# Sums with PSUM tiles of their own between projection and FFN, a shorter look-ahead there, and one empty unit in the first attention head

## The chip, the cores and the metric

The kernel runs on one core of one Trainium2 chip. The metric is the time of one execution on the device in microseconds (us), the median of several runs. One execution was recorded by the hardware profiler; all times of single instructions come from that one, counted in us from its first instruction. The engines are called PE (matrix products), PEld (its weight loads), DVE (vector engine), ACT (scalar engine), POOL (the general engine) and SP (here it only issues transfers).

## What is computed

One layer of a diffusion backbone on 384 tokens (128 context, 256 latent) of width 2048, all in float32:

```python
mod = silu(cond) @ w_ada + b_ada                 # six modulation vectors
h = rmsnorm(x) * (1 + sc1) + sh1
q, k, v, g, lr_f, lr_b, fo = split(h @ w_in)
la = log_sigmoid(lr @ w_a2 + b_a) / 16           # decays of each head, two directions
o = gla(q, k, v, la, states)                     # 4 heads, chunks of 64 tokens
f = real(fft2(fo))
m = (sigmoid(h @ w_gate + b_gate) halves: g_a * (o' @ w_br_gla) + g_b * (f @ w_br_four)) @ w_out
x = x + ga1 * rmsnorm(m)
h = rmsnorm(x) * (1 + sc2) + sh2
ff = (silu(h @ w_ffn_gate) * (h @ w_ffn_up)) @ w_ffn_down
x = x + ga2 * rmsnorm(ff)
```

## The kernel before

Activations lie transposed: a tile of 128 channels by T = 384 tokens, 16 such tiles (KT) for the width 2048. Every large product is made of three passes with operands split in a high and a low part (`hi*hi + hi*lo + lo*hi`, `gemm`, L254). A product of one output tile (`proj`, L263) takes two halves of 8 input tiles, each 24 matmuls of 128x384. Before each half `grab` takes a pair of split weights that lies ready and pushes a new one: a transfer on SP (`load`, L191), a cast on ACT (L224) and a subtraction on DVE (L225). The pairs are used three halves after they were pushed.

The order of instructions on PE, ACT, DVE and POOL is written out by hand (`manual_schedule`, L129): each engine executes its instructions in the order in which the program emits them. An instruction that waits holds up everything emitted behind it on its engine. Only SP's order is left to the scheduler.

**Gate products and GLA.** The loop at L817 makes 32 products of `w_gate`. After each half of a product it takes one step of a side job (`side`, L809): one unit of `gla()` and one of the modulation job `ada_rest` (two DVE operations L556 in most units). In the second half of a product the destination (`gate`, L818: ACT adds the bias and writes `gz`, L820; SP stores it) is emitted ahead of that step. `gla()` has 14 units for each of the four heads, cut by `yield`: unit 1 transposes k on PE (L635); unit 2 is the product for the decays, `z` (L650); unit 3 makes the decays from it, a chain over ACT (Abs L657, Exp L658, Ln L659), DVE (L661), ACT (cast `lah`, L284) and DVE (`lal`, L285); units 4 and 5 sum them on PE (`bT`, L671, and `sx`, L677) for the two directions and take their exponentials on ACT; units 6 to 14 do attention, states and outputs. Unit 1 of head 0 follows the first half of product 0. As 14 is even, each unit number keeps its place to first or second halves in all heads: unit 2 comes behind a second half and its `gz`, unit 3 behind a first half, unit 4 behind a second one. The loop has 64 steps; the four heads and three closing units take 59.

**From projection to FFN.** The loop at L1064 makes the 16 tiles of the output projection. `wout` (L1034) keeps running sums over the tiles in `qs[0..2]`: of squares, of the gated product with x, and of squares of the gated product. For the last tile `wout_last` (L1048) forms its terms straight from the product in PSUM, ACT and DVE by turns. Then `wide_sum` (L1101) sums over channels by matmuls with ones of 64 columns, DVE and ACT make two scale factors per token from the sums, and `rows2` (L1109) spreads each over 128 partitions (`prow`, `prow2`). With them `res_m` (DVE, L1133) and `res_a` (POOL, for tile 0 DVE, L1137) form the new x1, tile by tile, and `res_b` and `res_c` the input h2 of the FFN in a high and a low part: DVE, ACT, DVE. The first three FFN products are computed side by side while the tiles arrive (the "head", L1188 to L1204, 9 matmuls for each tile, L1201). `res_m` and `res_a` run LAG = 3 tiles ahead. After tiles 9 and 12 of that loop POOL gets a weight subtraction of 128x1024 (L1206). Three tiles (0, 9, 12) take a "fused" form in which the context and latent segments are scaled separately (L1161, L1165).

**The end.** `tok_sum` (L288) sums the squares of the FFN's output with one column of ones (L292); from them come the last scale, and 16 output tiles (L1278 to L1330).

PSUM is handed out from two pools of banks: `psm` (3, tag `mm`) and `pss` (5, tag `side`).

Of the kernel before, what the change touches and what calls it, by code (L numbers as in the profile page):

```python
# [96 lines left out]
def tile_step(ctx: ExitStack, tc: tile.TileContext, a, o):  # L97
# [498 lines left out]
    with ExitStack() as s:  # L596
# [23 lines left out]
        def gla():  # L620
# [10 lines left out]
            for h in range(NH):  # L631
# [30 lines left out]
                lah, lal = (pg.tile([P, 3, 2, P], F32R, tag=t, name=t) for t in ("lah", "lal"))  # L662
                split_act(lah, lal, la)
                yield
                for d in range(2):


                    bT = pss.tile([P, T], F32, tag="side", name="bT")
                    for t in range(3):
                        for j, l in enumerate((lah, lal)):  # L670
                            PE.matmul(  # L671
                                bT[:, t * P : (t + 1) * P], l[:, t, d], tri[:, d * P : (d + 1) * P],
                                start=j == 0, stop=j == 1,
                            )
# [344 lines left out]
    with ExitStack() as s:  # L1019
# [40 lines left out]
        rate[0] = 0.6  # L1060
        spare_h = ((pe, "hid_hi", 2), (pe, "hid_lo", 2))
# [2 lines left out]
        for i in range(KT):  # L1064
            p = psm.tile([P, T], F32, tag="mm", name="pmm")
            for g in range(2):
                n = 2 * i + g - 2 * KT
                if n < -6:
                    w = grab()
                else:  # L1070

                    w = take()
                    if raw2 is None:
                        raw2 = adap.tile([P, 2, G], F32, tag="adacc", name="raw2")
                    if n <= -4:
                        load(raw2[:, n % 2, :])
                    if n <= -5:
                        load()
                    split()
                    if -4 <= n <= -2:  # L1080
                        split(spare_w if n == -3 else spare_h)
                    if n >= -4:
                        load()
                    if n == -4:
                        load(raw2[:, 1, :])
                gemm(p, w, mT, 8, k0=8 * g, first=g == 0, last=g == 1)
                if g:
                    if i < KT - 1:
                        wout(p, i)
                    else:  # L1090
                        sq0, sq2 = wout_last(p, i)
# [9 lines left out]
        def wide_sum(dst, src):  # L1101
            for t in range(3):
                PE.matmul(dst[:, t, :], src[:, t * P : (t + 1) * P], ones[:, 0:64], start=True, stop=True)

        r = pe.tile([P, 2, 3], F32, name="r12", bufs=1)
        u = pe.tile([P, 2, 3], F32, name="u12", bufs=1)
# [9 lines left out]
        DVE.tensor_copy(u[:, 0, :], pst[0][:, 0, :, 0])  # L1116
# [4 lines left out]
        DVE.tensor_add(qs[2], qs[2], sq2)  # L1121
        wide_sum(pst[1][:, 1], qs[2])
        rows2(prow, 0)
        DVE.scalar_tensor_tensor(u[:, 0, :], pst[1][:, 1, :, 0], 0.5, r[:, 0, :], op0=ALU.mult, op1=ALU.mult)
        DVE.tensor_add(u[:, 0, :], u[:, 0, :], pst[1][:, 0, :, 0])
        DVE.scalar_tensor_tensor(u[:, 1, :], u[:, 0, :], 2.0 / D, r[:, 0, :], op0=ALU.mult, op1=ALU.mult)
        DVE.tensor_add(u[:, 1, :], u[:, 1, :], msx)

        t1s = {}

# [4 lines left out]
        def res_a(k):  # L1135

            (POOL if k else DVE).tensor_add(x1(k), t1s.pop(k), x1(k))  # L1137

        res_m(0)
        rsqrt(r[:, 1, :], u[:, 1, :], 1.0)  # L1140
        rows2(prow2, 1)
        for k in range(3):
            if k:
                res_m(k)
            res_a(k)
        for lo, hi, c in segs:
            DVE.tensor_scalar_mul(mg32(KT - 1)[:, lo:hi], p[:, lo:hi], mods[:, 2, KT - 1, c : c + 1])

        h2 = alloc_A()
        hp = [  # L1150
            (pss if u == 0 else psm).tile([P, T], F32, tag="mm" if u else "side", name="pmm") for u in range(HEAD)
        ]
        zt = [pss.tile([P, T], F32, tag="side", name="z") for _ in range(2)]
        fused = (0, 9, 12)

        def res_b(k):

            z = zt[k % 2]
            if k in fused:
                for lo, hi, c in segs:  # L1160
                    DVE.scalar_tensor_tensor(  # L1161
                        z[:, lo:hi], x1(k)[:, lo:hi], mods[:, 4, k, c : c + 1], prow2[:, lo:hi],
                        op0=ALU.mult, op1=ALU.mult,
                    )
                    ACT.activation(h2[0][:, k, lo:hi], z[:, lo:hi], AF.Identity, bias=mods[:, 3, k, c : c + 1])  # L1165
# [9 lines left out]
        def res_c(k):  # L1175
            z = zt[k % 2]
            if k in fused:
                for lo, hi, c in segs:
                    DVE.scalar_tensor_tensor(
                        h2[1][:, k, lo:hi], z[:, lo:hi], mods[:, 3, k, c : c + 1], h2[0][:, k, lo:hi].bitcast(F32),  # L1180
                        op0=ALU.add, op1=ALU.subtract,
                    )
# [104 lines left out]
        DVE.tensor_copy(r3, pst[:, 0:3])  # L1287
        DVE.tensor_add(r3, r3, pys[0][:, 0:3])
        rsqrt(r3, r3, 1.0 / D)
        put(pe_ks[0], psm, "mm")  # L1290
        for t in range(3):
# [117 lines left out]
```

## Time and profile before

| what | value |
|---|---|
| median of 3 runs | 2034.52 us (2034.43 to 2035.05) |
| the profiled execution, its own time | 2032.79 us |
| its span, first to last instruction | 2031.0 us |
| mean granted TensorE clock | 0.997 |
| busy DVE, ACT, POOL | 1251.2, 770.4, 34.2 us |

The page gives busy times and shares of the span; the view of waits says which engine sat idle until what; the timeline lists merged instructions with their start, their length and, in brackets, the idle time before them with what ended it; the view of windows gives for each stretch the busy time of each engine with the number of instructions, and the granted clock of TensorE, 1.00 for full speed.

### The profile page before, as it was taken

Reading aid. Unit: us, or ns where it says so; the run is one execution under the profiler, and the core shown is the slowest. Engines: PE = TensorE matmul, PEld = TensorE weight load, DVE = VectorE, ACT = ScalarE, POOL = GpSimd, SP = SyncE. Lnnn points to the kernel's source line nnn. Section 1 sums busy time; section 2 is a strip of 40 time slices with the busy share of each in tenths; the row PEclk is TensorE's granted clock in tenths of the full one; section 3 lists DMA queues with packets and bytes.
Section 4 is the critical chain, followed back from the end, with each engine's and each line's share of the span. In section 5 each row is a group of like instructions: output and inputs, shape, how many; then the busy total and the mean of one; then the engine's idle time right before and its main releaser. Section 6 shows DMA issues by size and latency. Waiting matters only on the chain.

```text
span 2031.0 us, 30079 instructions
## 1 busy us (share of the span) xinstructions
PE 2014.6 (99%) x12236; PEld 1959.9 (96%) x12236; DVE 1251.2 (62%) x1655; ACT 770.4 (38%) x1144; POOL 34.2 (2%) x46
## 2 busy tenths in 40 slices
PE   8999999999999999989999999999999999999999
PEld 5779999999999999989999999999999999999998
DVE  5669787898677778866444545453545454544345
ACT  4233545443346544446233222222222222222235
POOL 0000000000000000002000000000000000000001
PEclk9999999999999999999999999999999999999999
DMA  9978677767546785533444444443444444433332
GB/s 390 371 254 276 206 239 233 246 223 261 210 154 207 256 282 185 193 125 115 145 148 147 151 146 147 151 148 125 145 145 146 147 149 150 138 133 125 126 130 97
DMA packets 112395, 373.94 MB, mean 184 GB/s; under 512 B 13692, under 2 KB 32316, under 8 KB 108160
## 3 DMA queue, kind: packets, MB, share of 16 engines
q1 hardware_dynamic: 111248, 370.64, 53.2%
q8 instruction: 96, 1.57, 0.3%
q10 hardware_dynamic: 1008, 1.38, 0.2%
q14 instruction: 43, 0.35, 0.0%
HBM read 358.34 MB, written 13.63 MB: 183 GB/s over the span
## 4 chain that ended last, share of the span: by engine, by line
PE 98%; ACT 1%; DVE 1%; issue 0%; DMA 0%; ACTq 0%; DVEq 0%
PE pmm L258 67%; PE pdn L258 18%; PE pv L399 3%; PE pf L258 2%; PE pgm L382 1%; PE pmm L1201 1%; PE px L417 1%; PE px L300 0%; PE po L629 0%; PE pr L564 0%; PE py L1278 0%; PE pgm L496 0%; PE dl L629 0%; PE pp L856 0%; PE px L870 0%; PE bT L671 0%
## 5 line engine op out<-in xcount | busy, mean ns | idle before, releaser
L258 PE MATMUL pmm<-A_hi,whi 128*128 128x384 f32 x2480 | 831.8, 335 | 0.0
L258 PE MATMUL pmm<-A_hi,wlo 128*128 128x384 f32 x2480 | 828.9, 334 | 0.0
L258 PE MATMUL pmm<-A_lo,whi 128*128 128x384 f32 x2480 | 828.8, 334 | 0.0
L225 DVE TENSOR_TENSOR wlo<-raw,whi 128x1024 fp32r<-128x1024 f32 x434 | 529.8, 1223 | 416.8 <-ACT whi L224 415.6
L224 ACT CAST whi<-raw 128x1024 fp32r<-128x1024 f32 x436 | 457.5, 1050 | 582.4 <-PE pmm L258 226.9
L258 PEld LDWEIGHTS pmm<-A_hi,whi 128*128 128x128 f32 x2480 | 465.6, 188 | 2.9 <-issue 1.8
L258 PEld LDWEIGHTS pmm<-A_lo,whi 128*128 128x128 f32 x2480 | 465.7, 188 | 0.2
L258 PEld LDWEIGHTS pmm<-A_hi,wlo 128*128 128x128 f32 x2480 | 465.6, 188 | 0.0
L556 DVE SCALAR_TENSOR_TENSOR adacc<-adaw,spad,adacc 128x1024 f32<-128x1024 f32 x240 | 296.9, 1278 | 1.2 <-DMA adaw<-in_w_ada 1.0
L258 PE MATMUL pdn<-hid_hi,whi 128*128 128x384 f32 x704 | 235.2, 334 | 0.0
L258 PE MATMUL pdn<-hid_hi,wlo 128*128 128x384 f32 x704 | 235.1, 334 | 0.0
L258 PE MATMUL pdn<-hid_lo,whi 128*128 128x384 f32 x704 | 235.1, 334 | 0.0
L258 PEld LDWEIGHTS pdn<-hid_hi,whi 128*128 128x128 f32 x704 | 132.2, 188 | 0.4 <-issue 0.4
L258 PEld LDWEIGHTS pdn<-hid_lo,whi 128*128 128x128 f32 x704 | 132.2, 188 | 0.0
L258 PEld LDWEIGHTS pdn<-hid_hi,wlo 128*128 128x128 f32 x704 | 132.2, 188 | 0.0
L284 ACT CAST hid_hi<-hfE 128x384 fp32r<-128x384 f32 x44 | 22.6, 513 | 164.0 <-DVE hfE L1224 164.0
L1224 DVE TENSOR_TENSOR hfE<-sg,pmm 128x384 f32<-128x384 f32 x44 | 24.4, 555 | 84.6 <-PE pmm L258 84.0
L1216 ACT ACTIVATE sg<-pmm 128x384 f32<-128x384 f32 x44 | 21.6, 492 | 136.3 <-PE pmm L258 136.2
L1241 DVE TENSOR_TENSOR Blo<-Blo,pdn 128x384 f32<-128x384 f32 x72 | 39.5, 553 | 47.9 <-PE pdn L258 47.9
L1241 DVE TENSOR_TENSOR Bhi<-Bhi,pdn 128x384 f32<-128x384 f32 x72 | 39.1, 549 | 34.1 <-PE pdn L258 34.0
L258 PE MATMUL pmm<-o_hi,whi 128*128 128x384 f32 x128 | 42.8, 335 | 0.0
L258 PE MATMUL pmm<-o_lo,whi 128*128 128x384 f32 x128 | 42.8, 334 | 0.0
(309 smaller groups left out, 1520.9 us busy)
## 6 DMA issues: line engine op xcount, KB each, us to landing
adaw<-in_w_ada SPq DMA_DIRECT2D x128, 512.0 KB, 3.9
raw<-in_w_g SPq DMA_DIRECT2D x88, 512.0 KB, 3.2
raw<-in_w_u SPq DMA_DIRECT2D x88, 512.0 KB, 3.3
raw<-in_w_d SPq DMA_DIRECT2D x88, 512.0 KB, 3.2
slab<-in_w_ada SPq DMA_DIRECT2D x32, 1024.0 KB
raw<-in_w_gate SPq DMA_DIRECT2D x64, 512.0 KB, 4.5
raw<-in_w_in SPq DMA_DIRECT2D x44, 512.0 KB, 3.2
raw<-in_w_out SPq DMA_DIRECT2D x32, 512.0 KB, 4.5
```

What stands on the lines that cost most here:

```text
L224: ACT.copy(hi, raw)
L225: sub = lambda: eng.tensor_sub(lo, raw, hi.bitcast(F32))
L258: PE.matmul(dst, w[wi][:, k * n + n0 : k * n + n0 + P], x[xi][:, k0 + k, :], start=first and k == 0 and j == 0, stop=last and k == kts - 1 ...
L284: ACT.copy(hi, src)
L382: PE.matmul(pgv[q : q + 32, :], spad[:, k, :], slab[k // (KT // 2)][:, k % (KT // 2), :], start=k < 4, stop=k >= KT - 4,)
L399: PE.matmul(pv[2 * t + g], hT[x_][:, kb, t * P : (t + 1) * P], w_[:, g * 512 : (g + 1) * 512], start=kb == 0 and j == 0, stop=kb == KT - 1 ...
L417: PE.matmul(px, w_[:, u * P : (u + 1) * P], hT[x_][:, kb, :], start=j == 0, stop=j == 2)
L556: DVE.scalar_tensor_tensor(acc[:, c, :], w, spad[:, k, c : c + 1], acc[:, c, :], op0=ALU.mult, op1=ALU.add,)
L1201: PE.matmul(hp[u], hw[u][j][:, ((k - 1) % 8) * P : ((k - 1) % 8 + 1) * P], h2[m][:, k - 1, :], start=k == 1 and j == m == 0, stop=k == KT ...
L1216: ACT.activation(sgs[j], p, AF.Silu)
L1224: DVE.tensor_mul(hf, sgs.pop(j), p)
L1241: DVE.tensor_add(acc(k), acc(k), p)
```

## The change

In head 0 of `gla()` an empty unit follows the decay chain, so that `bT` and all that follows, in this head and the others, comes one step later. In the step from projection to FFN the last tile takes the way of the others (ACT writes `mg32`, squares it, DVE multiplies), but its terms are not added into `qs`: they get products of their own, and the four groups of sums (running and last, first and second factor) get four PSUM tiles. Small matmuls of ones by ones (`narrow_warm`) are put behind `prow` (2) and behind `prow2` (4); their result is never read. LAG becomes 2. In tile 0 the two segments go to different PSUM tiles (`zx` is new, from `psm`). At the end `tok_sum` is replaced by `wide_sum`.

```diff
                 split_act(lah, lal, la)
                 yield
+                if h == 0:
+                    yield
                 for d in range(2):
...
             for lo, hi, c in segs:
-                g = mods[:, 2, i, c : c + 1]
-                DVE.scalar_tensor_tensor(pr[:, lo:hi], p[:, lo:hi], g, x1(i)[:, lo:hi], op0=ALU.mult, op1=ALU.mult)
-                ACT.activation(sq2[:, lo:hi], p[:, lo:hi], AF.Square, scale=g)
-            DVE.tensor_add(qs[1], qs[1], pr)
-            return sq0, sq2
+                ACT.mul(mg32(i)[:, lo:hi], p[:, lo:hi], mods[:, 2, i, c : c + 1])
+            ACT.activation(sq2, mg32(i), AF.Square)
+            DVE.tensor_mul(pr, mg32(i), x1(i))
+            return sq0, pr, sq2
...
-        pst = [pss.tile([P, 2, 3, 64], F32, tag="side", name=f"pst{n}") for n in range(2)]
+        E0, S0, E12, S12 = (pss.tile([P, 2, 3, 64], F32, tag="side", name="pst") for _ in range(4))
...
-        wide_sum(pst[0][:, 0], qs[0])
-        DVE.tensor_copy(u[:, 0, :], pst[0][:, 0, :, 0])
-        wide_sum(pst[0][:, 1], sq0)
-        DVE.tensor_add(u[:, 0, :], u[:, 0, :], pst[0][:, 1, :, 0])
+        wide_sum(E0[:, 0], qs[0])
+        wide_sum(S0[:, 0], last3[0])
+        for n in (1, 2):
+            wide_sum(E12[:, n - 1], qs[n])
+        for n in (1, 2):
+            wide_sum(S12[:, n - 1], last3[n])
+        DVE.tensor_copy(e[:, 0, :], E0[:, 0, :, 0])
+        DVE.tensor_add(u[:, 0, :], e[:, 0, :], S0[:, 0, :, 0])
         rsqrt(r[:, 0, :], u[:, 0, :], 1.0 / D)
-        wide_sum(pst[1][:, 0], qs[1])
-        DVE.tensor_add(qs[2], qs[2], sq2)
-        wide_sum(pst[1][:, 1], qs[2])
         rows2(prow, 0)
...
+        def narrow_warm(n):
+            for _ in range(n):
+                PE.matmul(hp[1][:, 0:P], ones, ones, start=True, stop=True)
+
+        narrow_warm(2)
         res_m(0)
-        rsqrt(r[:, 1, :], u[:, 1, :], 1.0)
+        rsqrt(r[:, 1, :], u[:, 0, :], 1.0)
         rows2(prow2, 1)
-        for k in range(3):
+        narrow_warm(4)
+        LAG = 2
+        for k in range(LAG):
             if k:
                 res_m(k)
             res_a(k)
-        for lo, hi, c in segs:
-            DVE.tensor_scalar_mul(mg32(KT - 1)[:, lo:hi], p[:, lo:hi], mods[:, 2, KT - 1, c : c + 1])
...
+        zx = psm.tile([P, T], F32, tag="mm", name="zx")
...
+        def z_of(k, lo):
+
+            return zx if k == 0 and lo else zt[k % 2]
...
-        LAG = 3
...
-        tok_sum(pst[:, 0:3], qs[0], *late)
-        tok_sum(pys[0][:, 0:3], last_sq)
+        pst, ps2 = (t.rearrange("p (t c) -> p t c", t=3)[:, :, 0:64] for t in (pst, pys[0]))
+        wide_sum(pst, qs[0], *late)
+        wide_sum(ps2, last_sq)
```

More of the change, by code (lines that the diff above doesn't have):

```diff
@@ L1095, in tile_step, with wide_sum @@
                     pass
-        pst = [pss.tile([P, 2, 3, 64], F32, tag="side", name=f"pst{n}") for n in range(2)]
-        def wide_sum(dst, src):
+        E0, S0, E12, S12 = (pss.tile([P, 2, 3, 64], F32, tag="side", name="pst") for _ in range(4))
+        def wide_sum(dst, *src):
             for t in range(3):
-                PE.matmul(dst[:, t, :], src[:, t * P : (t + 1) * P], ones[:, 0:64], start=True, stop=True)
+                for n, x in enumerate(src):
+                    PE.matmul(
+                        dst[:, t, :], x[:, t * P : (t + 1) * P], ones[:, 0:64], start=n == 0, stop=n == len(src) - 1,
+                    )
         r = pe.tile([P, 2, 3], F32, name="r12", bufs=1)
-        u = pe.tile([P, 2, 3], F32, name="u12", bufs=1)
+        e = pe.tile([P, 3, 3], F32, name="e12", bufs=1)
+        u = pe.tile([P, 3, 3], F32, name="u12", bufs=1)
         prow, prow2 = (pss.tile([P, T], F32, tag="side", name="prow") for _ in range(2))
@@ L1113, in rows2 @@
                 )
-        wide_sum(pst[0][:, 0], qs[0])
-        DVE.tensor_copy(u[:, 0, :], pst[0][:, 0, :, 0])
-        wide_sum(pst[0][:, 1], sq0)
-        DVE.tensor_add(u[:, 0, :], u[:, 0, :], pst[0][:, 1, :, 0])
+        wide_sum(E0[:, 0], qs[0])
[6 more added lines that the diff above has]
+        DVE.tensor_add(u[:, 0, :], e[:, 0, :], S0[:, 0, :, 0])
         rsqrt(r[:, 0, :], u[:, 0, :], 1.0 / D)
-        wide_sum(pst[1][:, 0], qs[1])
-        DVE.tensor_add(qs[2], qs[2], sq2)
-        wide_sum(pst[1][:, 1], qs[2])
         rows2(prow, 0)
[L1124 to L1127, printed above, removed]
+        DVE.tensor_copy(e[:, 1:3, :], E12[:, :, :, 0])
+        DVE.tensor_add(u[:, 1:3, :], e[:, 1:3, :], S12[:, :, :, 0])
+        DVE.scalar_tensor_tensor(u[:, 2, :], u[:, 2, :], 0.5, r[:, 0, :], op0=ALU.mult, op1=ALU.mult)
+        DVE.tensor_add(u[:, 1, :], u[:, 1, :], u[:, 2, :])
+        DVE.scalar_tensor_tensor(u[:, 0, :], u[:, 1, :], 2.0 / D, r[:, 0, :], op0=ALU.mult, op1=ALU.mult)
+        DVE.tensor_add(u[:, 0, :], u[:, 0, :], msx)
         t1s = {}
@@ L1137, in res_a @@
             (POOL if k else DVE).tensor_add(x1(k), t1s.pop(k), x1(k))
+        hp = [
+            (pss if u == 0 else psm).tile([P, T], F32, tag="mm" if u else "side", name="pmm") for u in range(HEAD)
+        ]
+        def narrow_warm(n):
+            for _ in range(n):
+                PE.matmul(hp[1][:, 0:P], ones, ones, start=True, stop=True)
+        narrow_warm(2)
         res_m(0)
-        rsqrt(r[:, 1, :], u[:, 1, :], 1.0)
+        rsqrt(r[:, 1, :], u[:, 0, :], 1.0)
         rows2(prow2, 1)
-        for k in range(3):
+        narrow_warm(4)
+        LAG = 2
+        for k in range(LAG):
             if k:
@@ L1145, in tile_step @@
             res_a(k)
-        for lo, hi, c in segs:
-            DVE.tensor_scalar_mul(mg32(KT - 1)[:, lo:hi], p[:, lo:hi], mods[:, 2, KT - 1, c : c + 1])
         h2 = alloc_A()
-        hp = [
-            (pss if u == 0 else psm).tile([P, T], F32, tag="mm" if u else "side", name="pmm") for u in range(HEAD)
-        ]
         zt = [pss.tile([P, T], F32, tag="side", name="z") for _ in range(2)]
+        zx = psm.tile([P, T], F32, tag="mm", name="zx")
         fused = (0, 9, 12)
+        def z_of(k, lo):
+            return zx if k == 0 and lo else zt[k % 2]
         def res_b(k):
@@ L1160, in res_b @@
                 for lo, hi, c in segs:
+                    z = z_of(k, lo)
                     DVE.scalar_tensor_tensor(
@@ L1178, in res_c @@
                 for lo, hi, c in segs:
+                    z = z_of(k, lo)
                     DVE.scalar_tensor_tensor(
@@ L1283, in tile_step @@
         last_sq = late.pop()
-        tok_sum(pst[:, 0:3], qs[0], *late)
-        tok_sum(pys[0][:, 0:3], last_sq)
+        pst, ps2 = (t.rearrange("p (t c) -> p t c", t=3)[:, :, 0:64] for t in (pst, pys[0]))
+        wide_sum(pst, qs[0], *late)
+        wide_sum(ps2, last_sq)
         r3 = pe.tile([P, 3], F32, name="r3", bufs=1)
-        DVE.tensor_copy(r3, pst[:, 0:3])
-        DVE.tensor_add(r3, r3, pys[0][:, 0:3])
+        DVE.tensor_copy(r3, pst[:, :, 0])
+        DVE.tensor_add(r3, r3, ps2[:, :, 0])
         rsqrt(r3, r3, 1.0 / D)
```

2 lines of the change are left out of this document (1 added, 1 removed).

## The prediction

> **What bounds the kernel now.** I read the page first, then the view of waits of PE, then the timeline at each place where PE waits.
>
> ```profile
> span 2031.0 us, 30079 instructions
> PE 2014.6 (99%) x12236; PEld 1959.9 (96%) x12236; DVE 1251.2 (62%) x1655; ACT 770.4 (38%) x1144; POOL 34.2 (2%) x46
> ...
> PE 98%; ACT 1%; DVE 1%; issue 0%; DMA 0%; ACTq 0%; DVEq 0%
> ```
> ```profile
> PE pmm L1201 <- ACT A_hi L1165: 2.1, 1, 2.1
> PE pst L1103 <- DVE u L1116: 2.0, 1, 2.0
> PE prow L1111 <- DVE r L304: 0.8, 1, 0.8
> PE pst L1103 <- DVE qs L1121: 0.6, 1, 0.6
> ```
> ```profile
> PE bT L671 <- DVE lal L285: 0.7, 1, 0.7
> ```
>
> The chain that ended last is PE for 98%. So every microsecond that PE stands still is one at the end, and DVE's or ACT's time counts only where PE comes to wait for it. The change touches all five waits shown: four (5.5 us) lie between projection and FFN, one (0.7 us) in head 0's decays. I expect that it removes most of this and makes three longer waits elsewhere.
>
> **The empty unit.** This is the term that decides. The decay chain of head 1, in the timeline:
>
> ```profile
> 273.62 0.52 PE L649 MATMUL z<-cg 98*128 98x256 f32 x3
> 273.82 0.58 ACT L820 ACTIVATE gz<-pmm,bgate 128x384 f32<-128x384 f32 x1 [2.68 <-PE pmm L258]
> ...
> 275.24 0.87 ACT L657 ACTIVATE la<-z 128x512 f32<-128x512 f32 x2
> ...
> 281.16 0.96 DVE L285 TENSOR_TENSOR lal<-la,lah 128x768 fp32r<-128x768 f32 x1 [0.96 <-ACT lah L284]
> 282.04 2.48 DVE L556 SCALAR_TENSOR_TENSOR adacc<-adaw,spad,adacc 128x1024 f32<-128x1024 f32 x2
> 282.30 0.22 PE L671 MATMUL bT<-cg,lah 128*128 128x128 f32 x1
> ```
> ```profile
> 274.14 8.32 PE pmm L258 x48
> ```
> ```profile
> L659 ACT ACT_TABLE_LOAD x4 | 5.1, 1283 | 0.1
> ```
>
> From the first Abs to the end of `lal` are 281.16 + 0.96 - 275.24 = 6.88 us, each step waiting for the one before; the last row shows that the step in it, a table load of ACT ahead of Ln, comes once in each of the four heads and always takes 1.28 us. PE has two halves of a product between `z` and `bT`: 48 matmuls in 8.32 us, 4.16 a half. The chain ends at 282.12 and `bT` is due at 282.30: 0.18 us to spare. It fits because unit 3 is emitted behind a first half, where no `gz` stands ahead of it; ACT begins it 1.1 us after `z` ends (274.14), while PE is still at that half.
>
> One empty unit in head 0 makes 15 of its 14 units, so from its `bT` on, each unit changes from second to first halves or back. Heads 1 to 3 get `z` behind a first half and the chain behind a second half, thus behind `gz`, which needs the whole product. That ACT does stand still there, with work ready behind `gz`, shows in head 0:
>
> ```profile
> L717 PE MATMUL cr<-qi,kc x12: 222/222/222, 225.8 to 226.1; 128*64 128x64 f32 x12
> ```
> ```profile
> 236.18 0.58 ACT L820 ACTIVATE gz<-pmm,bgate 128x384 f32<-128x384 f32 x1 [3.58 <-PE pmm L258]
> 236.66 0.63 ACT L734 COPY att<-cr 64x192 f32<-64x192 f32 x2
> ```
>
> `cr` was finished at about 226.3, its copy ran at 236.66, right after a `gz` for which ACT had been idle 3.58 us. So in the changed order: `z` ends at 0, the second half ends on PE at 4.16; `gz` holds ACT for 0.58; the chain takes 6.88; `lal` is ready at 4.16 + 0.58 + 6.88 = 11.62. PE comes to `bT` at 8.32. **Stall 3.3 us, and 3.4 with 0.1 for handing over between the engines, in each of heads 1, 2 and 3: +10.2.** Behind the waiting `bT` in PE's queue stand `sx` and all later gate products, so nothing fills it. DVE waits inside the chain with its weight subtractions behind it, but a pair is used three halves (12.5 us) after it is pushed; I cost that at nothing, and if this reserve were gone, the two modulation operations ahead of them (2.48 us) would come on top at each head. Head 0 keeps its `z` and chain where they are and gets 4.16 us of reserve, so its wait goes: **-0.8** (0.7, and one weight load). Units 5 and 9 also move behind a `gz`. `bT` of unit 5 itself keeps PE 0.8 us behind the half's end, longer than `gz` takes, and unit 9's casts have a half of 4.16 us for work of some 2.5; both at nothing.
>
> **What the stalls do to the clock.** The view of windows, cut at the times at which the granted clock changes:
>
> ```profile
> 897.19:900.60 3.41, 1.84 (x14) 1.70 (x12) 1.15 (x3) 1.18 (x3) 0.00 (x0) 1.00 0.71 226
> 900.60:904.01 3.41, 2.39 (x19) 2.28 (x20) 1.09 (x5) 0.45 (x2) 0.00 (x0) 1.00 0.00 0
> 904.02:907.43 3.41, 2.59 (x13) 2.32 (x11) 2.73 (x10) 0.30 (x1) 0.17 (x1) 0.50 0.02 5
> 907.43:910.84 3.41, 1.34 (x5) 1.04 (x5) 2.98 (x9) 1.38 (x4) 2.78 (x3) 0.50 0.00 0
> 910.85:914.25 3.40, 3.40 (x12) 3.40 (x12) 3.31 (x7) 3.22 (x7) 2.03 (x2) 0.50 0.00 0
> 914.26:917.67 3.41, 3.41 (x21) 3.41 (x20) 3.31 (x8) 3.21 (x8) 2.15 (x3) 1.00 0.00 0
> ```
>
> The columns are the window, its length, PE, PEld, DVE, ACT and POOL busy with counts, the clock, DMA share and GB/s. The clock was halved for 10.2 us after the sums, from 904.02 to 914.26: three steps of 3.41. It fell after a window with 19 small matmuls (PE "busy" 2.39 of 3.41), and not after the one from 897.19, which had full products until 898.41 (the row stands further down) and then only 6 small ones. So a window with 1.2 us of full products keeps the clock, one with only short products loses it, and I put the limit at about 1.4 us of full products. A stall of 3.4 us leaves less than that in some window of 3.41 for (2 x 3.4 - 2 x 2.0) / 3.41 = 82% of the positions. Then the next window is at half speed; 12 matmuls against 21 in the rows of 910.85 and 914.26 lose 1.5 us, and a second window follows where the first still holds part of the stall. I take 1.6 for a head, **+4.8**, with 0 and 3 x 3.3 = 10 as ends.
>
> The Trainium skill ("TensorE: Matmul & The Clock Gate", Part 1) says that the clock is halved after one idle window of about 3.4 us, and that the windows run freely. By that rule a stall of 3.4 us beside full products leaves no window wholly idle, and this term would be 0. The rows above speak against it: the window before 904.02 was not idle at all. I follow the rows.
>
> **Projection to FFN.**
>
> ```profile
> 901.06 0.85 PE L1103 MATMUL pst<-ones,sq 128*128 128x64 f32 x6 [2.03 <-DVE u L1116]
> ...
> 906.12 1.62 PE L1111 MATMUL prow<-ident,r 128*128 128x128 f32 x6 [0.82 <-DVE r L304]
> ...
> 907.33 0.74 DVE L1147 TENSOR_SCALAR Blo<-pmm,mods 128x128 f32<-128x128 f32 x2
> 908.76 0.49 DVE L1161 SCALAR_TENSOR_TENSOR z<-Chi,mods,prow 128x256 f32<-128x256 f32 x1 [0.43 <-ACT A_hi L1165]
> ...
> 909.81 0.69 PE L1201 MATMUL pmm<-A_hi,whi 128*128 128x384 f32 x1 [2.07 <-ACT A_hi L1165]
> ```
>
> ```profile
> 898.08 0.33 PE L258 MATMUL pmm<-A_hi,wlo 128*128 128x384 f32 x1
> ```
>
> The last product ends at 898.41, the head starts 11.4 us later. Separate tiles take away the waits for `u` (2.0) and `qs` (0.6): ACT's square is ready about when the first six passes end. L1147 goes from ahead of the head (-0.7), the second segment of tile 0 no longer waits for ACT (-0.4). Two more sums are 12 passes at (0.85 - 0.28) / 5 = 0.11 each: +1.4. The sums and narrow products follow closely, so I take the clock to hold; the 12 passes of `prow`, about 0.21 apart at half clock, then take half: -1.3. Together the head starts -3.6 earlier. The narrow products (12 passes of 0.11 at full clock) lie where PE waits for `prow2`'s scalars and for tile 0: nothing; with half clock they would be 2.6 us, still within what was 0.8 + 2.1 of waits.
>
> In the head the tiles come from ACT and DVE as fast as PE uses them, and there LAG = 2 costs:
>
> ```profile
> 925.31 2.40 POOL L225 TENSOR_TENSOR wlo<-raw,whi 128x1024 fp32r<-128x1024 f32 x1
> 927.67 3.00 POOL L1137 TENSOR_TENSOR Clo<-t,Clo 128x384 f32<-128x384 f32 x3
> 930.63 2.39 POOL L225 TENSOR_TENSOR wlo<-raw,whi 128x1024 fp32r<-128x1024 f32 x1
> ```
> ```profile
> 932.27 0.56 DVE L1167 TENSOR_TENSOR z<-Clo,prow 128x384 f32<-128x384 f32 x1
> ```
>
> With LAG = 3 the add of tile 12 precedes the first big subtraction and that of tile 15 the second. With 2 both come behind. In today's times tile 15 would be added at 930.63 + 2.39 + 1.0 = 934.0, or 0.5 earlier as POOL then has one add less ahead of the subtraction: 1.2 after DVE reads it (932.27). I take about the same for tile 12 and 2.3 of lateness in all, which DVE, ACT and so PE feel. Start and lateness give **-1.3**; as the head's last tiles have little reserve to carry the whole 3.6, I take **-1.0**. Ends: -3.6 (the adds cost nothing) and +0.7 (the clock falls in the sums as it does now: `prow`'s 1.3 isn't gained, sums at half clock cost some 0.7 more, the adds 2.3).
>
> `zx` takes the last buffer of its pool. Its two readers are through early in the head, so the product after the head finds it free: nothing.
>
> **The end.**
>
> ```profile
> 2016.77:2020.17 3.40, 3.40 (x8) 1.94 (x7) 2.40 (x6) 0.48 (x1) 2.22 (x3) 0.50 0.00 0
> L292 PE MATMUL pstE<-ones,qsE x6: 166/250/250, 2013.1 to 2014.0; 128*128 128x1 f32 x6
> L1103 PE MATMUL pst<-ones,qs x18: 218/275/323, 898.3 to 903.8; 128*128 128x64 f32 x18
> ```
>
> A pass of 64 columns takes 25 ns more than one of a single column, at most 0.45 us over 18 passes, and overlaps with the next; I cost it at nothing. The wider passes may keep the clock that is now halved for these 3.4 us: **-0.5**, between +0.45 and half of 3.4.
>
> **Sum.** +10.2 - 0.8 + 4.8 - 1.0 - 0.5 = +12.7. The profiled execution took 2032.79 (span 2031.0 and 1.8 around it), which gives 2045.5; the median of the runs is 1.73 above it. I predict **2047 us**.
>
> **Rivals.**
> 1. *The stalls come, the clock stays*, because any full products in a window are enough. 10.2 - 0.8 - 1.0 - 0.5 = +7.9: 2042. For it: 1.2 us of them sufficed from 897.19 on. Against: most positions of a stall leave less. This is also the result by the page's rule.
> 2. *Not slower: `gz` doesn't hold the chain.* The place is ACT's queue between `gz` and Abs in heads 1 to 3. If Abs still starts up to 1.1 + 0.18 = 1.3 us after `z` ends, nothing waits; from there each microsecond later costs one. Then -0.8 - 1.0 - 0.5 = -2.3: 2032; with the adds free as well -4.9: 2030. Against it stands the copy at 236.66.
> 3. *Longer stalls*: DVE's reserve fails or two cold windows follow each stall: 12.7 + 5 or so: 2052 and more.
> 4. *The idle products don't do what they are for*, and the clock falls in the sums: +0.7 in place of -1.0, within the range.
>
> **How the numbers follow.** Forecast 0.53, rival 1 0.27, rival 2 0.13 (0.10 without a difference, 0.03 faster), rival 3 0.07. The measurement tells 0.2%, some 4 us, from no change; rivals 1 and 3 are on the slower side: slower 0.87, same 0.10, faster 0.03. The forecast's own range is 2044 to 2050; with rival 1 and part of rival 3 it is 2040 to 2052.
>
> **What would show it.** PE's waits must list `bT` for `lal` three times with 3 to 3.5 us, at heads 1 to 3 and not at head 0; Abs of these heads must start right after a `gz`. The clock of the windows behind them shows the second term. The waits for `u` and `qs` must be gone, the head must start 8 us after the last product in place of 11.4, and the DVE reads of tiles 12 and 15 must wait for POOL. If Abs starts ahead of `gz`, the prediction is wrong in its main step.

## The result, and the profile after

The changed kernel takes 2048.34 us (median of four runs, 2047.22 to 2050.02) against 2034.59 (2034.43 to 2035.05) for the kernel before beside it: ratio 1.0069, 95% interval 1.0057 to 1.0081. 2047 us had been predicted. The profiled execution took 2047.22 us.

The page after, first lines (busy time, share of the span, instructions) and the chain that ended last:

```profile
span 2045.4 us, 30121 instructions
...
PE 2021.9 (99%) x12260; PEld 1964.2 (96%) x12260; DVE 1250.3 (61%) x1652; ACT 770.3 (38%) x1145; POOL 34.1 (2%) x46
...
PE 96%; ACT 1%; DVE 1%; POOL 1%; issue 0%; DMA 0%; ACTq 0%; POOLq 0%; DVEq 0%
```

The span is 14.4 us longer, PE's busy time only 7.3 us: about half is PE standing still. The other half is mostly PE doing the same work more slowly, as the windows below show; only 24 short instructions are new. PE's share of the last chain falls from 98% to 96%, and POOL appears in it, which it did not before.

The view of waits of PE after (total us, times, longest):

```profile
PE bT L673 <- ACT lah L284: 6.8, 3, 2.3
...
PE bT L673 <- DVE lal L285: 2.0, 3, 0.7
PE pmm L1221 <- DVE A_lo L1205: 1.8, 2, 1.3
...
PE prow L1116 <- DVE r L304: 0.5, 1, 0.5
...
PE pmm L1221 <- ACT A_hi L1185: 0.5, 1, 0.5
```

The waits for `u` and `qs` are gone, those for `r` and the head's first tile are down from 0.8 and 2.1 to 0.5 and 0.5 us. Head 0's wait of 0.7 us for `lal` is gone too: the three in the view are those of heads 1 to 3. Two are new: `bT` waits three times, 8.8 us in all, first for `lah` and then for `lal`, and the head waits 1.8 us for `A_lo`.

The decay chain of head 1 after, in the timeline:

```profile
276.99 0.52 PE L649 MATMUL z<-cg 98*128 98x256 f32 x3
...
281.71 0.58 ACT L822 ACTIVATE gz<-pmm,bgate 128x384 f32<-128x384 f32 x1 [3.52 <-PE pmm L258]
282.19 0.86 ACT L657 ACTIVATE la<-z 128x512 f32<-128x512 f32 x2
...
285.50 0.34 PE L258 MATMUL pmm<-A_hi,wlo 128*128 128x384 f32 x1
...
288.10 0.96 DVE L285 TENSOR_TENSOR lal<-la,lah 128x768 fp32r<-128x768 f32 x1 [0.95 <-ACT lah L284]
288.12 0.33 PE L673 MATMUL bT<-cg,lah 128*128 128x128 f32 x1 [2.28 <-ACT lah L284]
289.11 0.33 PE L673 MATMUL bT<-cg,lal 128*128 128x128 f32 x1 [0.66 <-DVE lal L285]
...
290.04 0.52 PE L258 MATMUL pmm<-A_hi,whi 128*128 128x384 f32 x1
```

`z` ends at 277.51. ACT could run Abs from then on, but `gz` stands ahead of it and waits 3.52 us for PE; Abs starts right after it, at 282.19, that is 4.7 us after `z` in place of 1.1. From Abs to the end of `lal` are 289.06 - 282.19 = 6.87 us, as before (6.88). PE reaches the end of its two halves at 285.84 and stands. From the start of the last gate product to that of the next are 290.04 - 285.50 = 4.54 us. The same two products in the kernel before:

```profile
282.13 0.33 PE L258 MATMUL pmm<-A_hi,wlo 128*128 128x384 f32 x1
...
283.21 0.34 PE L258 MATMUL pmm<-A_hi,whi 128*128 128x384 f32 x1
```

1.08 us, with `bT` and `sx` between them: the stall takes 3.46 us of PE's time. The windows of the changed kernel around the three stalls (window, its length, PE, PEld, DVE, ACT and POOL busy with counts, granted clock, DMA share, GB/s):

```profile
286.54:289.95 3.41, 1.17 (x8) 1.03 (x9) 2.46 (x4) 2.70 (x3) 0.00 (x0) 1.00 0.00 0
289.95:293.36 3.41, 3.41 (x13) 3.41 (x13) 3.41 (x5) 2.44 (x5) 0.00 (x0) 0.50 0.27 82
...
358.22:361.63 3.41, 0.61 (x3) 0.19 (x1) 1.90 (x3) 2.27 (x3) 0.00 (x0) 1.00 0.00 0
361.63:368.45 6.82, 6.68 (x23) 6.68 (x24) 6.82 (x11) 3.41 (x6) 0.00 (x0) 0.50 0.43 141
...
433.31:436.72 3.41, 1.11 (x8) 0.97 (x8) 2.46 (x4) 2.64 (x3) 0.00 (x0) 1.00 0.00 0
436.73:440.14 3.41, 3.41 (x13) 3.41 (x13) 3.41 (x5) 2.49 (x5) 0.00 (x0) 0.50 0.23 61
```

After each stall the clock is halved, once for two windows: 13.65 us in all, in which PE shows busy almost throughout and does about half the work. This is the part of PE's longer busy time that no wait shows.

Where the span went, by start times of PE's instructions in the traces: the first transpose of k (`kr`, L635) of each head, the last product `po` of the GLA (L629), the first product `px` of the Fourier branch (L870), which follows the gate stage, the first sum, the first product of the FFN's head, the first product behind it, the first sum at the end (`pstE`), and the end.

| from, to | before, us | after, us | difference |
|---|---|---|---|
| head 0 | 68.65 | 71.77 | +3.12 |
| head 1 | 67.60 | 72.66 | +5.06 |
| head 2 | 67.41 | 74.17 | +6.75 |
| head 3, to the last `po` | 62.15 | 66.96 | +4.81 |
| last `po` to `px` | 55.69 | 51.53 | -4.16 |
| `px` to the first sum | 376.27 | 376.27 | 0.00 |
| first sum to the FFN's head | 11.56 | 8.24 | -3.32 |
| head to the next product | 27.10 | 29.47 | +2.37 |
| next product to `pstE` | 1076.20 | 1076.20 | 0.00 |
| `pstE` to the end | 17.86 | 17.44 | -0.42 |
| start to head 0 | 200.48 | 200.73 | +0.25 |

The -4.16 is no gain: the loop has 64 steps whatever the number of units, so the half product that the empty unit adds to head 0 is missing behind the last unit. Head 0's own gain is 3.12 - 4.16 = -1.04. The gate stage as a whole loses 15.58 us; everything after it gains 1.37.

Between projection and FFN, the changed kernel's timeline:

```profile
913.91 0.33 PE L258 MATMUL pmm<-A_hi,wlo 128*128 128x384 f32 x1
...
914.83 0.88 PE L1105 MATMUL pst<-ones,sq 128*128 128x64 f32 x6
...
920.07 0.91 PE L1116 MATMUL prow<-ident,r 128*128 128x128 f32 x6 [0.51 <-DVE r L304]
...
922.33 0.79 PE L1221 MATMUL pmm<-A_hi,whi 128*128 128x384 f32 x3 [0.45 <-ACT A_hi L1185]
```

The sums of the last tile follow the others without a wait, and the head starts 922.33 - 914.24 = 8.1 us after the last product's end. Then POOL's instructions, and two reads by DVE in the same stretch:

```profile
937.91 2.40 POOL L225 TENSOR_TENSOR wlo<-raw,whi 128x1024 fp32r<-128x1024 f32 x1
940.27 1.97 POOL L1145 TENSOR_TENSOR Clo<-t,Clo 128x384 f32<-128x384 f32 x2
...
944.57 2.39 POOL L225 TENSOR_TENSOR wlo<-raw,whi 128x1024 fp32r<-128x1024 f32 x1
946.92 1.01 POOL L1145 TENSOR_TENSOR Clo<-t,Clo 128x384 f32<-128x384 f32 x1
```
```profile
941.31 0.35 DVE L1181 SCALAR_TENSOR_TENSOR z<-Clo,mods,prow 128x128 f32<-128x128 f32 x1 [1.39 <-POOL Clo L1145]
...
947.96 0.56 DVE L1187 TENSOR_TENSOR z<-Clo,prow 128x384 f32<-128x384 f32 x1 [1.84 <-POOL Clo L1145]
```

Both adds now stand behind a big weight subtraction, and DVE waits 1.39 us for tile 12 and 1.84 us for tile 15. Most of it comes out at PE as the 1.8 us of waits for `A_lo`: of the 3.3 us that the earlier start gives, 2.4 are lost again in the head.

### The profile page after: what moved, and what is told of

Its sections match the earlier page's. It is cut to its first block, busy times and chain, and to the rows that moved or that the text cites. A ratio compares the mean times of both kernels' runs of the same rounds, so it can differ in the third digit from the quotient of the medians.

```text
span 2045.4 us, 30121 instructions
## 1 busy us (share of the span) xinstructions
PE 2021.9 (99%) x12260; PEld 1964.2 (96%) x12260; DVE 1250.3 (61%) x1652; ACT 770.3 (38%) x1145; POOL 34.1 (2%) x46
## 4 chain that ended last, share of the span: by engine, by line
PE 96%; ACT 1%; DVE 1%; POOL 1%; issue 0%; DMA 0%; ACTq 0%; POOLq 0%; DVEq 0%
PE pmm L258 66%; PE pdn L258 18%; PE pv L399 3%; PE pf L258 2%; PE pgm L382 1%; PE px L417 1%; PE px L300 0%; PE po L629 0%; PE pr L564 0%; PE bT L673 0%; POOL Clo L1145 0%; PE dl L629 0%; PE pgm L496 0%; PE pp L858 0%; PE px L872 0%
## 5 line engine op out<-in xcount | busy, mean ns | idle before, releaser
L822 ACT ACTIVATE gz<-pmm,bgate 128x384 f32<-128x384 f32 x32 | 18.6, 582 | 73.4 <-PE pmm L258 65.9
```

The costliest lines, as they stand in the source:

```text
L822: ACT.activation(g, p, AF.Identity, bias=bgate[:, i : i + 1])
```

## The experiments

The theory: the empty unit puts the decay chain of heads 1 to 3 behind a `gz` that needs the whole product, PE stands there, and the clock falls after each stall; the rest of the change is a gain of 1 to 3 us, and LAG = 2 takes part of it back. The rivals: the loss lies in the rest of the change; the unit as such, not its place, costs the time; the clock's fall costs nothing of its own; and, within the gain, the narrow products or the wider sums are not what holds the clock. All runs are in this table; lengths of heads 1 to 3 are differences to the kernel before, in us, from the traces.

| run | median, us | ratio, interval | heads 1, 2, 3 | sum to head | head to next | end |
|---|---|---|---|---|---|---|
| changed kernel | 2048.34 | 1.0069 [1.0057, 1.0081] | +5.06 +6.75 +4.81 | 8.24 | 29.47 | 17.44 |
| unit only | 2049.49 | 1.0074 [1.0059, 1.0089] | +5.09 +6.45 +4.81 | 12.34 | 27.32 | 17.36 |
| all but the unit | 2031.96 | 0.9988 [0.9978, 0.9997] | 0.00 0.00 0.00 | 8.24 | 29.50 | 17.43 |
| two units | 2031.92 | 0.9985 [0.9976, 0.9994] | +0.10 +0.21 -0.22 | 8.24 | 29.52 | 17.42 |
| `gz` behind | 2030.69 | 0.9984 [0.9975, 0.9994] | +0.05 +0.22 -0.22 | 8.24 | 29.48 | 17.42 |
| two units, LAG 3 | 2029.46 | 0.9974 [0.9963, 0.9984] | +0.10 +0.21 -0.22 | 8.50 | 26.62 | 17.43 |
| `gz` behind, LAG 3 | 2029.22 | 0.9972 [0.9962, 0.9983] | +0.05 +0.22 -0.22 | 8.49 | 26.67 | 17.42 |
| the same as "two units, LAG 3", no narrow products | 2029.43 | 0.9973 [0.9962, 0.9983] | +0.10 +0.21 -0.22 | 8.50 | 26.62 | 17.46 |
| the same, `tok_sum` at the end | 2029.32 | 0.9975 [0.9966, 0.9984] | +0.10 +0.21 -0.22 | 8.50 | 26.61 | 17.39 |
| stalls filled | 2040.93 | 1.0037 [1.0022, 1.0051] | +3.48 +3.68 +3.21 | 8.24 | 29.50 | 17.43 |

### The unit alone

The kernel before, with nothing but the empty unit:

```diff
                 yield
+                if h == 0:
+                    yield
                 for d in range(2):
```

> The kernel before with the empty unit of head 0 alone. Theory (the decay chain of heads 1 to 3 comes behind gz, and the clock falls after each stall): three waits of PE for lah and lal of 3.1 us together each (2.3 + 0.7 to 0.8), no wait in head 0, the clock halved once or twice behind each; 10.2 - 0.8 + 3 x (1.5 to 3) above before, 2048 to 2052. Rival (the loss of the changed kernel comes from the step to the FFN or from the two together): below 2040.

2049.49 us (2048.45 to 2050.49) against 2034.66. The waits of PE name the same two rows as in the changed kernel:

```profile
PE bT L673 <- ACT lah L284: 6.8, 3, 2.3
...
PE bT L673 <- DVE lal L285: 2.0, 3, 0.7
```

The whole loss is there with this one edit, in the same heads and with nearly the same lengths (16.35 us for the three in place of 16.62). That the rest of the change loses time falls as a rival. The longer stretch from the sums to the head (12.34 us in place of 11.56) has the old sums in it, and in this execution the clock was halved there for four windows, where the old profile has three.

### All but the unit

The changed kernel without these two lines.

```diff
                 yield
-                if h == 0:
-                    yield
                 for d in range(2):
```

> The changed kernel without the empty unit. Theory: the step to the FFN and the end give -3.3 + 2.4 - 0.4 = -1.3, so 2033.3, no wait for lah, and the old wait of 0.7 for lal in head 0. Rival as for the unit alone: 2043 or more.

2031.96 us (2031.37 to 2033.61), 2.7 below the median before, where 2033.3 had been expected. Heads 1 to 3 are as before to 0.01 us. The parts that the rest of the change touches give -3.32 + 2.40 - 0.43 = -1.35 us, as expected. The median fell by twice that; the mean clock of the executions of before, 0.995 or 0.996 in most, is below the 0.997 of the profiled one, so that the profile may show less of the old kernel's half clock than most executions had. In the profile of this run PE waits 0.41 us for DVE at 706.43, and the part from `px` to the first sum is 0.87 us longer; no other trace here has that, and I take it for chance. The rest of the change is worth about 0.1% with LAG = 2.

### The same number of halves again: two units

Is it the unit, or its oddness? With two, head 0 has 16 units, and heads 1 to 3 get their places back.

```diff
                 if h == 0:
                     yield
+                    yield
                 for d in range(2):
```

> The changed kernel with two empty units in head 0 in place of one. Theory (only the place to first or second halves counts): no wait for lah or lal in any head, head 0's wait gone, 2033.3 - 0.8 to 1.0 = 2032.4. Rival (a later unit collides with the modulation job, PSUM or the weights, the more the later it is): waits in heads 1 to 3 as with one unit or longer, 2045 or more.

2031.92 us (2030.43 to 2032.21). The waits of PE have no row for `bT`. The largest behind the start of the kernel is that of LAG = 2:

```profile
PE pmm L1222 <- DVE A_lo L1206: 1.8, 2, 1.3
```

Twice the delay costs nothing where one costs 14 us. What decides is whether unit 2 is emitted behind a second half or a first one, and with it the chain of unit 3 behind a first half or behind a `gz`. Head 0 keeps the gain: its length is +7.34, two halves of 4.16 less 0.98, as against 4.16 less 1.04 with one unit.

### One unit, `gz` out of the way

The changed kernel, with the read of a finished gate product emitted behind the step of the side jobs, so that the chain's ACT instructions come ahead of `gz` in ACT's queue. The places of all units stay as changed.

```diff
-    def proj(pool, x, dst, side=None):
+    def proj(pool, x, dst, side=None, ahead=False):
...
-            if g:
+            if g and not ahead:
                 dst(p)
             step(side)
+            if g and ahead:
+                dst(p)
...
-            proj(psm, hT, gate, sd)
+            proj(psm, hT, gate, sd, ahead=True)
```

> The changed kernel, one empty unit, but in the gate products gz is emitted behind the step of the side jobs and not ahead of it. Theory (it is gz that holds ACT): Abs of heads 1 to 3 starts while PE is still in the second half, the chain ends before bT, no wait for lah or lal in heads 1 to 3, 2032 to 2034. Rival (the chain is late for another reason, DVE or its own length): the waits stay at 2 us or more each, 2042 or more.

2030.69 us (2030.22 to 2032.88), somewhat less than expected. The chain of head 1 in this kernel's timeline:

```profile
276.83 0.52 PE L651 MATMUL z<-cg 98*128 98x256 f32 x3
277.82 0.86 ACT L659 ACTIVATE la<-z 128x512 f32<-128x512 f32 x2
...
283.60 0.58 ACT L824 ACTIVATE gz<-pmm,bgate 128x384 f32<-128x384 f32 x1
283.72 0.96 DVE L287 TENSOR_TENSOR lal<-la,lah 128x768 fp32r<-128x768 f32 x1 [0.95 <-ACT lah L286]
...
285.51 0.22 PE L675 MATMUL bT<-cg,lah 128*128 128x128 f32 x1
```

Abs starts 0.47 us after `z` ends, `lal` is ready at 284.68, 0.83 us before PE asks for it, and `gz` can wait: it starts some 2 us after its product is done (277.35 and a half product of 4.16 make 281.5), and the three heads lose nothing by it. This takes away the one thing that the theory names and leaves the empty unit in, so the cause is shown: ACT's place for `gz`, not the delay.

### The stalls left in, but filled

The stall and the clock's fall behind it come together in the changed kernel. Here PE gets 14 matmuls of ones by ones (28 passes) ahead of `bT` in heads 1 to 3, whose result is not read; the chain is as late as in the changed kernel.

```diff
                 yield
+                if h:
+                    idle = pss.tile([P, T], F32, tag="side", name="idle")
+                    for _ in range(14):
+                        PE.matmul(idle[:, 0:P], ones, ones, start=True, stop=True)
                 for d in range(2):
```

> The changed kernel with 14 idle products of ones by ones (28 passes of 0.11, 3.0 together) ahead of bT in heads 1 to 3; their result is never read. The chain and so bT come no earlier. Theory (after the stalls the clock falls, and that is a cost of its own): the waits for lah shrink to below 0.5, the end of the stall stays, but the clock is no longer halved at 290, 362 and 437; 1.5 to 6 less than the changed kernel, 2043 to 2046.5. Rival (the clock's falls cost nothing, since PE runs ahead of ACT and DVE there anyway): 2048 to 2049.

2040.93 us (2040.82 to 2041.11) against 2033.26 for the kernel before beside it, ratio 1.0037 in place of 1.0069: by the ratios 6.5 us less than the changed kernel, a little more than the 1.5 to 6 expected. The rival, that the clock's falls cost nothing, falls. Timeline and windows at head 1:

```profile
285.63 0.34 PE L258 MATMUL pmm<-A_hi,wlo 128*128 128x384 f32 x1
285.81 3.29 PE L670 MATMUL idle<-ones 128*128 128x128 f32 x28
...
289.24 0.33 PE L677 MATMUL bT<-cg,lal 128*128 128x128 f32 x1
```
```profile
285.00:288.30 3.30, 3.30 (x29) 3.30 (x28) 1.10 (x3) 2.14 (x4) 0.00 (x0) 1.00 0.00 0
288.30:292.00 3.70, 3.61 (x27) 3.47 (x26) 3.70 (x4) 3.67 (x6) 0.00 (x0) 1.00 0.00 0
```

The `bT` for `lal` starts 289.24 - 285.63 = 3.61 us after the last product in this kernel and 289.11 - 285.50 = 3.61 in the changed one, so filling does not lengthen the stall itself; at head 2 the same two numbers are 3.61 as well. The clock stays at 1.00, and the three heads lose 3.48 + 3.68 + 3.21 = 10.37 us in place of 16.62. This parts the two: the stalls cost 10.37, the clock behind them 6.25. That fits the 13.65 us at half clock, which can cost 6.8 at most.

### LAG 3 again

The kernel with two units, and LAG as before the change.

```diff
-        LAG = 2
+        LAG = 3
```

> Two empty units in head 0 and LAG = 3, all else as in the changed kernel. Theory (with LAG = 2 the adds of tiles 12 and 15 stand behind POOL's two weight subtractions): DVE no longer waits for POOL at tiles 12 and 15 (1.39 and 1.84 in the changed kernel), PE's waits for A_lo of 1.8 go, the head takes 27.1 or less in place of 29.5, 2031.9 - 2.4 = 2029.5. Rival (the head is bound by ACT's work for each tile, whatever the order of the adds): the head stays at 29, 2031.5 or more.

2029.46 us (2027.96 to 2030.12). POOL's order in this kernel, at the first big subtraction and the adds around it:

```profile
922.97 2.40 POOL L225 TENSOR_TENSOR wlo<-raw,whi 128x1024 fp32r<-128x1024 f32 x1
925.32 3.00 POOL L1146 TENSOR_TENSOR Clo<-t,Clo 128x384 f32<-128x384 f32 x3
928.29 2.39 POOL L225 TENSOR_TENSOR wlo<-raw,whi 128x1024 fp32r<-128x1024 f32 x1
```

Three adds stand between the two subtractions and none behind the second, as in the kernel before; PE's waits for `A_lo` are gone. The head takes 26.62 us in place of 29.52 and starts 0.26 later, since three tiles instead of two come ahead of it: LAG = 2 costs 2.6 us by the profiles, 2.5 by the medians.

The same with the other cure, one unit with `gz` behind the step:

> One empty unit, gz behind the step, and LAG = 3. Theory: both costs of the change gone, 2030.7 - 2.4 = 2028.3, the fastest of all. Rival as for the run with two units and LAG = 3: 2030.5.

2029.22 us (2027.80 to 2029.51). It had been expected as the fastest of all, from the difference between the two cures at LAG = 2 (2031.92 and 2030.69); at LAG = 3 the two cannot be told apart, so that difference was not one of the cures. Both beat the kernel before by 5 us (0.26 and 0.28%), and the changed kernel by 19.

### No narrow products

Two units, LAG 3, without the six small matmuls.

```diff
-        narrow_warm(2)
         res_m(0)
         rsqrt(r[:, 1, :], u[:, 0, :], 1.0)
         rows2(prow2, 1)
-        narrow_warm(4)
```

> As the run with two empty units and LAG = 3, but without the six narrow products. What is left out is never read. Theory (short products must fill a window, or the clock falls): the window that holds prow and prow2 loses half of its products, the clock falls ahead of the head in most executions, rows and head start slower, 1 to 2.5 more. Rival (the sums packed together suffice): the clock holds and the time is that of the run with them.

2029.43 us (2027.86 to 2029.61), the same as with them: the theory fails, the rival holds. In each trace here the clock changes only at times that are whole multiples of 3.413 us apart (326 of them lie between 904.02 and 2016.77 in the kernel before), so that it can be said where the windows lie in which it is decided. In this kernel the clock falls at 2023.80, near the end, and 329 steps ahead of that a window begins at 900.81. The windows over the sums and the start of the head are these:

```profile
900.81:904.23 3.42, 2.46 (x22) 2.29 (x20) 2.23 (x9) 0.30 (x1) 0.00 (x0) 1.00 0.00 0
904.23:907.64 3.41, 1.81 (x11) 1.47 (x9) 3.41 (x10) 1.93 (x5) 2.99 (x4) 1.00 0.00 0
```

The clock stays at 1.00 through both and behind them, though the first holds only sums and `prow` and the second has PE busy for 1.81 us of 3.41. PE waits longer in the views of waits (1.6 us for `A_hi`, 1.0 for `r`, in place of 0.7 and 0.5), which only means that the narrow products had filled waits; the head starts at the same 8.50 us. The narrow products do nothing here that can be measured. In all nine profiles with separate tiles for the sums the clock holds there, in both with the old sums (before, and the unit alone) it falls. So the closely packed sums are enough; how far apart they could lie was not tested.

### `tok_sum` at the end

Two units, LAG 3, with the single-column sums at the end that the change had replaced.

```diff
-        pst, ps2 = (t.rearrange("p (t c) -> p t c", t=3)[:, :, 0:64] for t in (pst, pys[0]))
-        wide_sum(pst, qs[0], *late)
-        wide_sum(ps2, last_sq)
+        tok_sum(pst[:, 0:3], qs[0], *late)
+        tok_sum(pys[0][:, 0:3], last_sq)
...
-        DVE.tensor_copy(r3, pst[:, :, 0])
-        DVE.tensor_add(r3, r3, ps2[:, :, 0])
+        DVE.tensor_copy(r3, pst[:, 0:3])
+        DVE.tensor_add(r3, r3, pys[0][:, 0:3])
```

> As the run with two empty units and LAG = 3, but with sums of one column at the end as before. Theory (the wider passes keep the clock): the clock is halved in the stretch after the sums and the end takes 17.9 in place of 17.4, 0.4 more. Rival (the width makes no difference): the end takes 17.4.

2029.32 us (2027.95 to 2030.66), end 17.39 us. The stretch behind its sums, in its windows:

```profile
2012.00:2016.00 4.00, 3.96 (x18) 2.34 (x19) 1.74 (x6) 0.78 (x2) 1.23 (x2) 1.00 0.00 2
```

The clock stays without wide sums, and the kernel with the unit alone, which also has `tok_sum`, ends in 17.36 us. The medians show no difference, and the expected 17.9 us did not come. But where the clock's windows lie differs from execution to execution, and one pair of profiles has them alike. The window over the sums begins 0.25 us after the first sum starts in the kernel before (single columns, first line) and 0.30 us after it in the kernel without the unit (64 columns, second line).

```profile
2013.36:2016.76 3.40, 3.36 (x24) 2.66 (x24) 1.56 (x5) 1.10 (x3) 0.00 (x0) 1.00 0.01 2
2013.58:2016.99 3.41, 3.32 (x24) 2.62 (x23) 1.50 (x5) 1.10 (x3) 0.00 (x0) 1.00 0.01 2
```

Both windows hold 24 instructions; behind the first the clock was halved for 3.4 us and the end took 17.86 us, behind the second it stayed. So by this one pair the width can decide where the windows lie unluckily; in the other two profiles with single columns they lay elsewhere. What it is worth on average, these runs are too few to show.

## Why the prediction was right

The forecast had 12.7 us by its terms; the profiled executions differ by 14.43 (2032.79 to 2047.22). The median stood 1.1 us above the profiled execution in place of the 1.73 assumed, so that of the 1.7 us that the sum was short 1.3 show in the median.

| term | predicted | measured | from |
|---|---|---|---|
| stalls of heads 1 to 3 | +10.2 | +10.4 | filled stalls, heads 1 to 3 |
| head 0's wait | -0.8 | -1.0 | 3.12 - 4.16 |
| clock behind the stalls | +4.8 | +6.25 | 16.62 - 10.37 |
| projection to FFN | -1.0 | -0.95 | 2.37 - 3.32 |
| the end | -0.5 | -0.4 | 17.44 - 17.86 |
| start | none | +0.25 | 200.73 - 200.48 |

- **The place of the stall** was read right. From the place of unit 2 in the halves and from ACT's idle time ahead of a `gz` in the old profile, the prediction put three stalls of 3.4 us at heads 1 to 3, with Abs right behind `gz`; the trace shows them there with 3.46 us at head 1, and putting `gz` behind the chain removes all three. One sign was off in its form: the view of waits was to list `bT` for `lal` with 3 to 3.5 us. It lists 2.3 us for `lah` and 0.7 for `lal`, since the first pass of `bT` needs only `lah`, and PE runs that pass in between. Rival 2 (Abs still starts early) falls with the row of 282.19. DVE's reserve held: the stalls are no longer than the chain, so rival 3's first half falls too.
- **The clock term was mis-sized**: +4.8 by 1.6 for a head, measured +6.25. Heads 1 and 3 cost about that, 5.06 - 3.48 = 1.58 and 4.81 - 3.21 = 1.60. Head 2 costs 6.75 - 3.68 = 3.07, since its clock stays halved for two windows. Its stall fell almost wholly into one window (358.22 to 361.63, PE busy 0.61), and by the timeline `bT` and `sx` still run at the start of the next one, at half clock. The prediction had named a second window and put only 0.1 us on it (1.6 in place of the 1.5 of one window). It also took 82% for the chance that a stall loses the clock; in the two profiles with unfilled stalls all six did. Two steps behind the 82% were off. It measured by full products and counted the stall alone, but `bT` and `sx` behind it are no full products either: from the last full product to the next are 290.04 - 285.84 = 4.2 us, and the windows from 286.54 and 433.31 hold no full product at all. And it put the limit at 1.4 us of full products, although its own row from 897.19 had kept the clock with 1.2.
- **The clock rule.** The windows ahead of the three falls have PE busy for 1.17, 0.61 and 1.11 us. Rival 1 held that any full products in a window are enough. The kernel with the unit alone speaks against it: its window at head 2 has 0.87 us of full products, up to 358.12, and the clock fell behind it:

```profile
357.25:360.66 3.41, 1.13 (x7) 0.74 (x5) 1.30 (x3) 2.25 (x4) 0.00 (x0) 1.00 0.00 0
```

The Trainium skill ("TensorE: Matmul & The Clock Gate", Part 1) has the clock halved after an idle window of about 3.4 us, by which the result would have been that of rival 1, 2042 us. The rows differ from it: no window ahead of these falls was idle, and the price is the 6.25 us above. What the Trainium skill says there of the windows, that they run freely, agrees with the trace: the halved stretches are 3.41 us long or twice that, and they start 71.68 and 75.10 us apart, which is 21 and 22 times 3.413.
- **Projection to FFN** came out at -0.95 with both halves as priced, -3.3 at the start (predicted -3.6) and +2.4 from LAG (2.3), at tiles 12 and 15. One step of it fell: short products alone were said to lose the clock, and the narrow ones were counted among what holds it. The window from 900.81 of the kernel without narrow products has only sums and `prow` in it and keeps the clock.
- **The end** came out in the profile at the size forecast, with some luck: that the old sums lose the clock there was read from one execution, and two others with single columns kept it. That the wider passes can keep it has one pair of windows for it; the medians with and without them are the same.

## What to carry to other kernels

Where side work is dealt out in steps between the halves of a product, a step's place counts as much as its lateness: before you shift one, write down for each engine what then stands ahead of it in the queue and when that can run. One more step cost 14 us here, two cost nothing, and emitting the read of the finished product behind the step cost nothing either. When PE stalls for about the 3.4 us of a clock window, add the half-speed windows behind it to the bill (here 6 us on 10); filling the stall with products nobody reads saves that part alone, getting rid of the wait saves both.

## What the runs showed of the hardware that had not been expected

**Busy time of PE does not tell whether a window keeps the clock.** The window of the old kernel from 900.60, 2.39 us busy with 19 short instructions, was followed by half clock, and so was the one from 2013.36, 3.36 us busy; that of the kernel without narrow products from 904.23, 1.81 us busy with 11, was not. This one holds the first products of the head. But the one from 900.81, 2.46 us busy with 22 short instructions and no full product, kept the clock as well. It has 10 passes of 64 columns and 12 of 128, the lost one from 900.60 has 18 of 64 and one of 128; and of the pair at the end the wider passes kept it. This fits a count of the columns that pass through, rather than of busy time; no run here was made to test it, and what is counted stays open.

**Executions of one kernel fall in groups, the lower two about 1.4 us apart.** The runs of the kernel before lie near 2033.2, 2034.6 or 2035.6, those of the kernel with two units and LAG 3 near 2028.0, 2029.5 or 2030.1. Two profiles of nearly the same kernel, with and without narrow products, at 20 to 25 us:

```profile
20.00:25.00 5.00, 3.69 (x13) 2.90 (x17) 2.84 (x6) 0.67 (x2) 0.00 (x0) 0.66 1.03 416
```
```profile
20.00:25.00 5.00, 3.64 (x37) 2.54 (x41) 3.44 (x7) 0.71 (x2) 0.00 (x0) 1.00 1.01 410
```

The first, from an execution of 2029.53 us, has one window at half clock there and reaches head 0 at 202.09 us; the second, from one of 2028.12 us, has none and reaches it at 200.63. In these two the 1.46 us account for the whole difference of 1.41. The other profiles agree: the four with such a window (two units, with LAG 2 and 3; `gz` behind with LAG 3; `tok_sum`) reach head 0 at 201.9 to 202.1 us, the seven without it at 200.3 to 200.9. That every run of an upper group has it was not recorded, and what makes the third group is not known. At LAG = 2 most runs of both cures lie near 2030.5 or near 2032, four and six of ten with two units, six and three of ten with `gz` behind. Their medians fell into different groups: the 1.2 us that seemed to part them.

**The spread.** The five runs with filled stalls lie within 0.3 us, the four of the changed kernel within 2.8. With the stalls filled, the clock in heads 1 to 3 no longer depends on where its windows lie; but five runs may also all fall in one group, so this is a hint and no more.
